# Attention probabilities kept side by side and turned in place, in a block of projections, dilated attention and HGRN2

## The chip, the cores and the metric

The kernel runs on one core of one Trainium2 chip. The metric is the device time of one execution in microseconds; lower is better. Engines are called as the profile calls them: PE is TensorE's matmuls and PEld its weight loads, DVE is VectorE, ACT is ScalarE, POOL is GpSimd, and SP issues most DMAs.

## What is computed

One layer of a hybrid encoder on 1024 tokens of width 1024, all in float32:

```
h = layer_norm(x)
aq, ak, av, hq, hf_fwd, hf_bwd, hi, hg, ga, gh = split(h @ w_in)          # 11776 columns
att = dilated_attention(aq, ak, av)    # 3 groups of 8 heads of 64: windows 128, 512, 2048 at dilation 1, 4, 16
rec = hgrn2(hq, hf_fwd, hf_bwd, hi, hg)   # 8 heads of 128: two gated linear recurrences, in chunks of 64
m = sigmoid(ga) * (att @ w_att_up) + sigmoid(gh) * (rec @ w_hgrn_up)
h = layer_norm(alpha * h + m @ w_o)
out = layer_norm(alpha * h + (silu(gate) * up) @ w_ffn_out)               # gate, up = split(h @ w_ffn_in)
```

Each attention group is a banded softmax with a linear bias in the distance. The three groups of a head are mixed with weights made of their softmax denominators: with each group's probabilities p, their row maximum and their row sum l, the output is the sum over the groups of w_g * (p_g @ v_g), where w_g holds one factor per query, exp(smallest shift - shift_g) over the common denominator.

HGRN2 has for each head and direction a cumulated product of the forget gate within a chunk, queries and keys scaled by it and by its reciprocal, a state that is carried from chunk to chunk, and the outputs of both directions added.

## The kernel before

The program has three phases. The change touches the first alone, `phase1`, which makes all 11776 columns of the input projection and, in between, the attention and the recurrences.

**The stream of products.** `stream` makes the projection in a Strassen-like form: groups of four 128-column tiles, 14 products for each group, 322 in all. A product is 12 matmuls of 128x512 (`mm3`, lines 225 to 227: high x high, high x low, low x high parts of float32 in TensorE's float32r type). Each needs a weight block split into a high part on ACT (line 200) and a low part on POOL (line 204); blocks are loaded by SP one group ahead. Results go through four PSUM banks (`ps_pj`); ACT and DVE take them out, and SP stores them to scratch in DRAM.

**Side work.** While the stream runs, the loop at the end of `phase1` advances one generator at a time: a unit of side work. `yield n` means: go on after n more products; a negative number also lets the next unit's inputs be fetched (`hgrn_pre`, `att_pre`, `near_pre`). For each i of 0 to 3 the units are two HGRN2 heads (`hgrn_side`), the far attention of a pair of heads (`att_far`, dilations 4 and 16) and the near attention of that pair (`att_near`, dilation 1). A unit begins when the stream has made the tiles that it reads. The order in the program is not exactly that of the code: instructions are ordered by priority, which is the order of the code save for evictions of the stream (`high_priority`), and by the program's own estimate of when their inputs are there. Side work has four PSUM banks of its own (`ps_sd`), used in turn, and nine SBUF slots of 4 KB a partition (`slot`).

**Far attention.** Scores of dilation 4 for 8 blocks (4 rounds r, 2 halves h) of 128 queries and 192 keys (line 565), and of dilation 16 for 128 queries and 128 keys (line 581), with bias and row maximum in one DVE instruction (line 517). A block's 320 numbers stand side by side; 16 exponentials follow (line 595). Then, for each round, `turn` transposes: of dilation 16 four full 128x128 blocks for each of the two heads in every other round (line 614), and of dilation 4, for each head, a full block (619), a half-width piece of one half (620), a half-width piece of the other half by a plain matmul into the lower partitions (621), and a full block (622). `att_pt` copies each bank to a fresh buffer, on ACT or DVE. The output matmuls of the round follow (633, 638, 642), and the next round's `turn` behind them. At the end `to_rows0` (line 661) brings the negated maxima N12 and the sums L12 into the row order of the near unit, in two passes of four matmuls with 16 columns.

**Near attention.** Scores of eight row tiles (line 696; tile 0 has two 64-row pieces), exponentials (715), the mixing weights W12 and W0 (lines 722 to 731), a broadcast of each on POOL (733), transposes (748 to 754) with copies, output matmuls (785). `weigh` transposes a broadcast weight (764) and multiplies: the far output OL and a copy ON of the near output are weighted apart and then added on POOL (796).

**A head of HGRN2.** `hgrn_dir` makes for each direction the gates, two scans (858), two reciprocals of 512 columns (866, 869) and the scaled queries and keys. Then: turn v; turn the keys of direction 0 (`hgrn_keys`, 884, 885); its state matmuls and state chain (`hgrn_states`, 900 to 912, the chain on DVE as hR and on ACT as hS); the same for direction 1; scores (`hgrn_scores`, 925 to 929) and outputs (`hgrn_out`, 951) for the two halves; the transposed store.

A plain float32 matmul shows as two PE instructions in the trace, a transpose as one.

Of the kernel before, what the change touches and what calls it, by code (L numbers as in the profile page):

```python
# [75 lines left out]
SMT_PAD = 640  # L76
# [3 lines left out]
class Block:  # L80
# [458 lines left out]
    FAR = [(s, o) for s in (2, 3, 4, 5, 8) for o in range(3)] + [(9, 0)]  # L539
# [5 lines left out]
    def att_far(self, j, qk):  # L545
# [3 lines left out]
        M1, M2, M12, N12, L12 = (self.att_small(n) for n in ("M1", "M2", "M12", "N12", "L12"))  # L549
# [3 lines left out]
        tiles = {n: self.slot(n, "pf", (3, 320)) for n in (2, 3, 4, 5, 8)}  # L553
        tiles[9] = self.smt.tile([128, 1, 320], F32, name="pf", tag="pf", bufs=1)

        def P(c, hd):
            s, o = self.FAR[2 * c + hd]
            return tiles[s][:, o, :]

        yield 2  # L560
        for r in range(4):
# [5 lines left out]
            for hd, ps in enumerate(pss):  # L567
                for h in range(2):
                    s, c = slice(192 * h, 192 * h + 192), 2 * r + h
                    self.ttr(P(c, hd)[:, 0:192], ps[:, s], bias[hd][:, s], M1[:, hd, c:c + 1])  # L570
            if r % 2:
                yield 1
        k2 = k2.rearrange("p (h r i m) -> p r i h m", h=2, r=4, i=4)
        for b in range(2):
# [8 lines left out]
            for hd, ps in enumerate(pss):  # L583
                for jj in range(4):
                    c, h = 4 * b + jj, jj % 2
                    self.ttr(P(c, hd)[:, 192:320], ps[:, jj, :], bias2[hd][:, 128 * h:128 * h + 128], M2[:, hd, c:c + 1])
            if b == 0:
                yield 1
# [14 lines left out]
        self.turned(V2, lambda kt: V2[:, kt, :])  # L603
        yield 1

        kw = dict(skip_group_check=True)
        t2 = {}

        def turn(r):
            if r % 2 == 0:  # L610
                for hd in range(2):
                    ps = self.ps_sd()
                    for jj in range(4):
                        nc.tensor.transpose(ps[:, 128 * jj:128 * jj + 128], P(2 * r + jj, hd)[:, 192:320], ident)
                    t2[hd] = self.att_pt(ps, 0, 512, hd).rearrange("p (r h c) -> p r h c", r=2, h=2)
            t = []
            for hd in range(2):
                ps, a, b = self.ps_sd(), P(2 * r, hd), P(2 * r + 1, hd)
                nc.tensor.transpose(ps[:, 0:128], a[:, 0:128], ident)
                nc.tensor.transpose(ps[0:64, 128:256], a[:, 128:192], ident)  # L620
                nc.tensor.matmul(ps[64:128, 128:256], b[:, 0:64], ident, start=True, stop=True)
                nc.tensor.transpose(ps[:, 256:384], b[:, 64:192], ident)
                t.append(self.att_pt(ps, 0, 384, hd))
            return t

        t = turn(0)
        yield 1
        O = [self.ps_sd(), self.ps_sd()]
        for r in range(4):
            o = [[O[h][HD[hd], 128 * r:128 * r + 128] for hd in range(2)] for h in range(2)]  # L630
            for h in range(2):
                for hd in range(2):
                    nc.tensor.matmul(o[h][hd], V1[:, 2 * r + h, HD[hd]], t[hd][:, 256 * h:256 * h + 128],
# [870 lines left out]
```

## Time and profile before

| | before |
|---|---|
| runs, median of 3 | 2222.41 us (2219.23 to 2223.08) |
| the profiled execution | 2221.32 us, span 2219.5 us |
| TensorE's mean granted clock | 0.98 |
| `w_lo` splits on POOL for the projection's blocks (line 204, wa) | 276, 1383 ns each |
| reciprocals of HGRN2 (lines 866 and 869) | 32, 3328 and 3333 ns each |
| exponentials of the far units (line 595) | 64, 551 ns each |

How to read it: the page gives the busy time of each engine, the chain of work that ended last, and groups of instructions by line with their mean length. Matmuls are pipelined, so the length of one (0.39 us for a product's matmul) is more than the time between two of them (0.23 us). The durations used below are taken from one profiled execution and set against that execution's own 2221.32 us.

### The profile page before, as it was taken

To read this page: it belongs to the slowest core of one execution; us is meant where nothing else is said; L and a number is where in the kernel's file an instruction comes from. 1 tells how busy PE (TensorE), PEld (TensorE's weight loads), DVE (VectorE), ACT (ScalarE), POOL (GpSimd) and SP (SyncE) were. 2 spreads that over 40 slices of the span, in tenths; PEclk is the share of its full clock that TensorE was granted. 3 is DMA by queue.
4 is the path that set the end of the run, shared out by engine and by line. 5 is a ranking of instruction groups with operands and counts; after the bars stand their busy time and mean duration, and the time that the engine had idled before them with its cause. 6 is when DMAs were issued, how large, how long until landed. Compare 5 with 4: busy or idle time off the path is not lost.

```text
span 2219.5 us, 30900 instructions
## 1 busy us (share of the span) xinstructions
PE 2111.7 (95%) x11105; PEld 1713.1 (77%) x11105; DVE 1223.2 (55%) x1917; ACT 883.2 (40%) x1744; POOL 1124.1 (51%) x911
## 2 busy tenths in 40 slices
PE   4799999998999999989999899998999999999998
PEld 3678877787777887777877788786788888887887
DVE  7666534785338852678424723248667676743221
ACT  6544445443544435544355432133444444432000
POOL 3465643665436763466543664446556665633120
PEclk9899999999999999999999999999999999999999
DMA  6333432434324443333432774334434443467453
GB/s 208 104 119 114 145 119 96 133 115 143 121 91 133 133 150 101 127 115 117 152 100 81 268 240 155 100 128 140 154 118 139 130 146 129 142 214 218 128 166 95
DMA packets 291643, 306.87 MB, mean 138 GB/s; under 512 B 14689, under 2 KB 222882, under 8 KB 291490
## 3 DMA queue, kind: packets, MB, share of 16 engines
q1 hardware_dynamic: 283744, 278.45, 39.7%
q10 hardware_dynamic: 7746, 26.45, 3.1%
q8 instruction: 87, 1.43, 0.3%
q14 instruction: 66, 0.54, 0.1%
HBM read 203.13 MB, written 101.71 MB: 137 GB/s over the span
## 4 chain that ended last, share of the span: by engine, by line
PE 66%; DVE 6%; DMA 4%; issue 3%; POOL 2%; ACT 1%; SPq 0%; DVEq 0%; ACTq 0%; POOLq 0%
PE pj L227 14%; PE pj L225 14%; PE pj L226 13%; PE sd L225 6%; PE sd L227 6%; PE sd L226 6%; DMA w_raw<-in_w_ffn_out_dram 2%; PE sd L951 1%; POOL w_lo L204 1%; PE sd L696 1%; DVE hR L912 1%; DMA t_raw<-td 1%; PE sd L785 1%; DVE wolo L204 1%; PE sd L509 1%
## 5 line engine op out<-in xcount | busy, mean ns | idle before, releaser
L204 POOL TENSOR_TENSOR w_lo<-wa,w_hi 128x512 fp32r<-128x512 f32 x276 | 379.9, 1383 | 318.1 <-ACT w_hi L200 294.2
L200 ACT CAST w_hi<-wa 128x512 fp32r<-128x512 f32 x276 | 170.3, 618 | 266.7 <-PE pj L226 193.6
L204 POOL TENSOR_TENSOR w_lo<-wsum,w_hi 128x512 fp32r<-128x512 f32 x88 | 122.0, 1398 | 129.3 <-ACT w_hi L200 77.4
L225 PE MATMUL pj<-xt1hi,w_hi 128*128 128x512 f32 x268 | 109.3, 408 | 27.2 <-ACT xt1hi L200 22.5
L204 POOL TENSOR_TENSOR w_lo<-f_raw,w_hi 128x512 fp32r<-128x512 f32 x66 | 99.7, 1511 | 46.2 <-ACT w_hi L200 43.9
L227 PE MATMUL pj<-xt1hi,w_lo 128*128 128x512 f32 x268 | 108.3, 405 | 1.9 <-POOL w_lo L204 1.9
L226 PE MATMUL pj<-xt1lo,w_hi 128*128 128x512 f32 x268 | 108.3, 404 | 0.3 <-DVE xt1lo L204 0.3
L225 PE MATMUL pj<-xb22hi,w_hi 128*128 128x512 f32 x268 | 105.8, 395 | 0.1
L227 PE MATMUL pj<-xb22hi,w_lo 128*128 128x512 f32 x268 | 105.8, 395 | 0.0
L226 PE MATMUL pj<-xb22lo,w_hi 128*128 128x512 f32 x268 | 104.9, 391 | 0.0
L200 ACT CAST w_hi<-wsum 128x512 fp32r<-128x512 f32 x88 | 54.6, 621 | 109.5 <-PE sd L226 74.3
L194 POOL TENSOR_TENSOR mv<-mv,mhalf 128x1 f32<-128x1 f32 x24 | 14.0, 586 | 165.2 <-DVE mv L193 164.2
L415 POOL TENSOR_TENSOR wa<-wa,wa 128x512 f32<-128x512 f32 x46 | 64.3, 1399 | 62.5 <-DVE ws L414 48.7
L204 POOL TENSOR_TENSOR w_lo<-ws,w_hi 128x512 fp32r<-128x512 f32 x46 | 65.2, 1419 | 60.7 <-ACT w_hi L200 53.0
L437 ACT COPY wkeep<-pj 128x512 f32<-128x512 f32 x138 | 80.2, 582 | 19.2 <-DVE evh L356 8.2
L225 PE MATMUL pj<-xb11hi,w_hi 128*128 128x512 f32 x188 | 76.3, 407 | 7.9 <-ACT xb11hi L200 7.9
L225 PEld LDWEIGHTS pj<-xt1hi,w_hi 128*128 128x128 f32 x268 | 52.3, 195 | 40.5 <-ACT xt1hi L200 23.0
L329 DVE TENSOR_TENSOR evh<-wkeep,pj 128x512 f32<-128x512 f32 x66 | 58.3, 886 | 44.3 <-PE pj L227 35.9
L903 ACT ACTIVATE hS<-hR,dec 128x128 f32<-128x128 f32 x112 | 44.6, 403 | 84.5 <-DVE hR L912 51.1
L225 PE MATMUL pj<-xt2hi,w_hi 128*128 128x512 f32 x188 | 74.8, 399 | 3.3 <-ACT w_hi L200 2.4
L225 PE MATMUL pj<-xt4hi,w_hi 128*128 128x512 f32 x188 | 75.3, 401 | 1.7 <-DVE wkeep L354 1.7
L248 ACT ACTIVATE y<-y,mv 128x1024 f32<-128x1024 f32 x14 | 17.3, 1244 | 148.3 <-DVE mv L247 93.1
(399 smaller groups left out, 6605.4 us busy)
## 6 DMA issues: line engine op xcount, KB each, us to landing
wa<-in_w_in_dram SPq DMA_DIRECT2D x184, 256.0 KB, 3.0
f_raw<-in_w_ffn_in_dram SPq DMA_DIRECT2D x44, 512.0 KB, 4.0
w_raw<-in_w_ffn_out_dram SPq DMA_DIRECT2D x22, 512.0 KB, 3.7
tg<-evh SPq DMA_DIRECT2D x32, 256.0 KB, 3.5
tg<-tg SPq DMA_DIRECT2D x16, 512.0 KB, 4.1
y<-ahs SPq DMA_DIRECT2D x16, 512.0 KB, 4.0
ah<-xt ACTq DMA_DIRECT2D x8, 512.0 KB, 4.6
rec<-hg ACTq DMA_DIRECT2D x8, 512.0 KB, 2.7
```

The costliest lines, as they stand in the source:

```text
L200: nc.scalar.copy(hi, src)
L204: e.tensor_sub(lo, src, hi.bitcast(F32))
L225: nc.tensor.matmul(ps, whi, xhi, start=first, stop=False, **kw)
L226: nc.tensor.matmul(ps, whi, xlo, start=False, stop=False, **kw)
L227: nc.tensor.matmul(ps, wlo, xhi, start=False, stop=last, **kw)
L329: nc.vector.tensor_tensor(o, self.order_src(add, g, kind), s, OP.add)
L415: nc.gpsimd.tensor_sub(a["a21"], a["a11"], a["a21"])
L437: nc.scalar.copy(t, ps)
L509: nc.tensor.transpose(ps[:, 128 * k:128 * (k + 1)], cols(4 * b + k), self.ident)
L696: nc.tensor.matmul(ps[:, tt % 2, :], q[pb, 128 * tt - 64:128 * tt + 64], k[pb, 128 * (tt - 1):128 * (tt + 1)], start=True, stop=True)
L785: nc.tensor.matmul(O[bank][HD[hd], c0:c1], V[:, kt, HD[hd]], t[hd][:, s0:s0 + c1 - c0], start=first, stop=(kt == 7), **kw)
L903: nc.scalar.activation(S[:, c, :], E, AF.Copy, scale=dec[:, 1, c:c + 1])
```

## The change

Three things are done.

In the far units a round's probabilities of dilation 4 stand side by side as 384 columns for both halves, with dilation 16 on either side of them where the slot has room (then one exponential still covers 320 columns) and in the upper part of another slot where not (then two exponentials, their sums added through LB). They are turned as full 128x128 blocks, three for dilation 4 and two for dilation 16, and copied back over themselves. All transposes come first, in three steps, and all outputs in one step. N12 and L12 are one tile NL and go through `to_rows0` in one pass of 32 columns.

In the near units the weight W0 is multiplied into the probabilities before they are turned, the weight W12 alone is broadcast and turned, the unused quarters of tile 0 are set to zero so that all its blocks are full, and the outputs are made row tile by row tile in one step. OL is multiplied by the turned weight and the outputs are added to it from PSUM.

In the heads, `hgrn_dir` is a generator: each direction is emitted in two parts, with a product between the parts and between the directions. Reciprocals are made in two halves. v and the keys of direction 0 are turned in one step, the keys of direction 1 go with the states of direction 0, and the two halves of scores, of outputs and of the last transposes each go in one step.

```diff
-    def att_pt(self, ps, c0, c1, i):
-        t = self.half("pt")
+    def copied(self, i, o, s):
         if i % 2:
-            self.nc.scalar.copy(t[:, c0:c1], ps[:, c0:c1])
+            self.nc.scalar.copy(o, s)
         else:
-            self.nc.vector.tensor_copy(t[:, c0:c1], ps[:, c0:c1])
-        return t
+            self.nc.vector.tensor_copy(o, s)
...
-    FAR = [(s, o) for s in (2, 3, 4, 5, 8) for o in range(3)] + [(9, 0)]
+    FAR = [(s, 128, s, 0) for s in (2, 3, 4, 5, 8)] + [(2, 640, 5, 640), (3, 640, 8, 640), (4, 640, 9, 0)]
...
-        for c in range(8):
+        for r in range(4):
             for hd in range(2):
-                v = P(c, hd)
-                nc.scalar.activation(v, v, AF.Exp, bias=N12[:, hd, c:c + 1], scale=QSCALE, accum_out=L12[:, hd, c:c + 1])
-        v1, v2 = self.fetch(0, "v1", d["v", 1], True), self.fetch(1, "v2", d["v", 2])
+                s1, _, s2, _ = self.FAR[2 * r + hd]
+                for h in range(2):
+                    c = 2 * r + h
+                    if s1 == s2:
+                        todo = [(tiles[s1][:, 320 * h:320 * h + 320], L12)]
+                    else:
+                        todo = [(P1(r, hd)[:, 192 * h:192 * h + 192], L12), (P2(r, hd)[:, h], LB)]
+                    for v, l in todo:
+                        nc.scalar.activation(v, v, AF.Exp, bias=N12[:, hd, c:c + 1], scale=QSCALE,
+                                             accum_out=l[:, hd, c:c + 1])
+        nc.vector.tensor_add(L12, L12, LB)
...
+        def turn1(r):
+            for hd in range(2):
+                ps, p = self.ps_sd(), P1(r, hd)
+                for n in range(3):
+                    nc.tensor.transpose(ps[:, 128 * n:128 * n + 128], p[:, 128 * n:128 * n + 128], ident)
+                self.copied(hd, p, ps[:, 0:384])
+
+        def turn2(r0):
+            for hd in range(2):
+                ps = self.ps_sd().rearrange("p (r e c) -> p r e c", r=2, e=2)
+                for r in range(2):
+                    for e in range(2):
+                        nc.tensor.transpose(ps[:, r, e], P2(r0 + r, hd)[:, e], ident)
+                for r in range(2):
+                    self.copied(hd, P2(r0 + r, hd), ps[:, r])
+
+        turn1(0)
+        turn1(1)
         yield 1
+        turn1(2)
+        turn2(0)
+        yield 1
+        turn1(3)
+        turn2(2)
+        perm = self.half("perm")
+        nc.sync.dma_start(perm, self.tabs[:, 128:640])
+        yield 2
...
-            if r < 3:
-                t = turn(r + 1)
-                yield -1 if r == 1 else 1
...
+        self.far = None, *self.to_rows0(perm, NL)
...
-        RB = []
-        for n, w in ((1, W12), (2, W0)):
+        for w in (W0, W12):
             nc.vector.tensor_mul(w, w, L0)
-            RB.append(self.slot(n, "rb", (8, 2, 64)))
-            nc.gpsimd.tensor_copy(RB[-1], w.rearrange("p a t -> p t a")[:, :, :, None].to_broadcast([128, 8, 2, 64]))
-        yield 1
+
+        RB = self.slot(1, "rb", (8, 2, 64))
+        nc.gpsimd.tensor_copy(RB, W12.rearrange("p a t -> p t a")[:, :, :, None].to_broadcast([128, 8, 2, 64]))
+        for tt in range(8):
+            for hd in range(2):
+                for p, z in rows(tt, hd):
+                    nc.vector.tensor_scalar(z, z, W0[p, hd, tt:tt + 1], None, op0=OP.mult)
+        yield 2
...
+        for b in range(4):
             for hd in range(2):
                 ps = self.ps_sd()
...
+                for tt in (2 * b, 2 * b + 1):
+                    for e in (0, 128):
+                        o = 256 * (tt % 2) + e
+                        nc.tensor.transpose(ps[:, o:o + 128], tile(tt, hd)[:, e:e + 128], ident)
+                self.copied(hd, P[b][:, hd].rearrange("p t c -> p (t c)"), ps)
+            if b % 2:
+                yield b
...
         for b, src, dst in cols:
-            nc.scalar.copy(ON[:, dst], O[b][:, src])
+            nc.vector.tensor_mul(OL[:, dst], OL[:, dst], RL[b][:, src])
+        for b, src, dst in cols:
+            nc.vector.tensor_add(OL[:, dst], OL[:, dst], O[b][:, src])
+        nc.scalar.dma_start(self.att_d[j], OL)
         yield -1
-        weigh(1, ON)
-        nc.gpsimd.tensor_add(OL, OL, ON)
-        nc.scalar.dma_start(self.att_d[j], OL)
...
-        nc.vector.reciprocal(qd[:, :, far], A)
         nc.gpsimd.tensor_mul(t3[:, :, near], t3[:, :, near], R)
+        yield
+        for c in (slice(0, 4), slice(4, 8)):
+            nc.vector.reciprocal(qd[:, c, far], A[:, c])
...
-            self.hgrn_dir(h, d, st)
+            for _ in self.hgrn_dir(h, d, st):
+                yield 1
+            if d == 0:
+                yield 1
         sg = self.fetch(8, "hg", self.hg_d[h]["g"])
+        yield 1
+        vT = self.turned(v.rearrange("p (k d) -> p k d", k=8), lambda c: v[:, 128 * c:128 * c + 128])
+        k0 = self.hgrn_keys(st, 0)
+        yield 3
+        S = {0: self.hgrn_states(st, 0, k0, vT)}
+        k1 = self.hgrn_keys(st, 1)
+        yield 3
+        S[1] = self.hgrn_states(st, 1, k1, vT)
+        yield 3
+        am = [self.hgrn_scores(st, b) for b in range(2)]
+        yield -2
+        on = [self.hgrn_out(st, b, am[b], vT, S) for b in range(2)]
         yield 2
...
```

More of the change, by code (lines that the diff above doesn't have):

```diff
@@ L552, in att_far, with P1, P2 @@
         bias, bias2 = self.att_bias(j, 1), self.att_bias(j, 2)
[L553 to L558, printed above, removed]
+        tiles = {n: self.slot(n, "pf") for n in (2, 3, 4, 5, 8)}
+        tiles[9] = self.smt.tile([128, 256], F32, name="pf", tag="pf", bufs=1)
+        nc.gpsimd.memset(LB, 0.0)
+        def P1(r, hd):
+            s, o = self.FAR[2 * r + hd][:2]
+            return tiles[s][:, o:o + 384]
+        def P2(r, hd):
+            s1, _, s, o = self.FAR[2 * r + hd]
+            if s1 != s:
+                return tiles[s][:, o:o + 256].rearrange("p (e c) -> p e c", e=2)
+            return tiles[s][:, 0:1024].rearrange("p (e c) -> p e c", e=2)[:, :, 0:128]
         yield 2
@@ L603, in att_far @@
         self.turned(V2, lambda kt: V2[:, kt, :])
-        yield 1
-        kw = dict(skip_group_check=True)
[L607 to L627, printed above, removed]
+        yield 2
[15 more added lines that the diff above has]
+        turn1(1)
+        yield 1
+        turn1(2)
[5 more added lines that the diff above has]
+        nc.sync.dma_start(perm, self.tabs[:, 128:640])
+        yield 2
+        kw = dict(skip_group_check=True)
         O = [self.ps_sd(), self.ps_sd()]
@@ L652, in att_far, with to_rows0 @@
             nc.scalar.copy(dst, O[h].rearrange("p (r i u) -> p r i u", r=4, i=4))
-        yield 1
-        self.far = OL, self.to_rows0(perm, N12, "N12r"), self.to_rows0(perm, L12, "L12r")
-    def to_rows0(self, perm, src, name):
+        self.far = OL, *self.far[1:]
+        yield -1
+    def to_rows0(self, perm, src):
         nc = self.nc
@@ L758, in att_near @@
-        cols = ((0, slice(64, 512), slice(0, 448)), (1, slice(0, 512), slice(448, 960)), (0, slice(0, 64), slice(960, 1024)))
-        def weigh(i, o):
-            RL = [self.ps_sd(), self.ps_sd()]
-            for tt in range(8):
-                c = 128 * (tt % 4)
-                nc.tensor.transpose(RL[tt // 4][:, c:c + 128], RB[i][:, tt].rearrange("p a d -> p (a d)"), ident)
-            for b, src, dst in cols:
-                nc.vector.tensor_mul(o[:, dst], o[:, dst], RL[b][:, src])
-        t = turn(0)
@@ L769, in att_near @@
-        yield 1
-        O = [self.ps_sd(), self.ps_sd()]
-        for b in range(4):
-            for kt in (2 * b, 2 * b + 1):
-                o = 256 * (kt % 2)
-                c = 128 * (kt % 4)
-                if kt == 0:
-                    parts = [(0, 64, 256, 64, True)]
-                elif kt == 3:
-                    parts = [(0, 384, 512, 256, False), (1, 0, 128, 384, True)]
-                elif kt == 7:
-                    parts = [(1, 384, 512, 256, False), (0, 0, 64, 384, False)]
-                else:
-                    parts = [(kt // 4, c, c + 256, o, False)]
-                for bank, c0, c1, s0, first in parts:
-                    for hd in range(2):
-                        nc.tensor.matmul(O[bank][HD[hd], c0:c1], V[:, kt, HD[hd]], t[hd][:, s0:s0 + c1 - c0],
-                                         start=first, stop=(kt == 7), **kw)
-            if b < 3:
-                t = turn(b + 1)
-                yield 1
@@ L790, in att_near @@
-        weigh(0, OL)
-        ON = self.slot(6, "on")
+                for tt in (2 * b, 2 * b + 1):
[5 more added lines that the diff above has]
+                yield b
+        RL = [self.ps_sd(), self.ps_sd()]
+        for tt in range(8):
+            c = 128 * (tt % 4)
+            nc.tensor.transpose(RL[tt // 4][:, c:c + 128], RB[:, tt].rearrange("p a d -> p (a d)"), ident)
@@ new lines, in att_near @@
+        O = [self.ps_sd(), self.ps_sd()]
+        todo = []
+        for kt in range(8):
+            c = 128 * (kt % 4)
+            todo.append((kt, O[kt // 4], c + (64 if kt == 0 else 0), c + 128, kt, 192 if kt == 0 else 128))
+            t = kt + 1
+            todo.append((kt, O[t % 8 // 4], 128 * (t % 4), 128 * (t % 4) + (64 if t == 8 else 128), t % 8, 0))
+        begun = set()
+        for n, (kt, o, c0, c1, t, p0) in enumerate(todo):
+            for hd in range(2):
+                first, last = id(o) not in begun, all(id(z[1]) != id(o) for z in todo[n + 1:])
+                nc.tensor.matmul(o[HD[hd], c0:c1], V[:, kt, HD[hd]], tile(t, hd)[:, p0:p0 + c1 - c0],
+                                 start=first, stop=last, **kw)
+            begun.add(id(o))
```

97 lines of the change are left out of this document (36 added, 61 removed).

## The prediction

> **What bounds the kernel now.** I read the page's busy line and its chain first, then the table of stages in the stretch where the changed code runs (122 to 1222 us), then TensorE's waits, then TensorE's timeline, because a sum of busy times cannot price short matmuls that overlap one another.
>
> ```profile
> span 2219.5 us, 30900 instructions
> PE 2111.7 (95%) x11105; PEld 1713.1 (77%) x11105; DVE 1223.2 (55%) x1917; ACT 883.2 (40%) x1744; POOL 1124.1 (51%) x911
> ...
> PE 66%; DVE 6%; DMA 4%; issue 3%; POOL 2%; ACT 1%; SPq 0%; DVEq 0%; ACTq 0%; POOLq 0%
> ...
> 122.00:276.00 154.00, 150.21 (x884) 126.50 (x882) 95.78 (x130) 66.69 (x132) 93.60 (x85) 0.99 0.42 132
> 276.00:405.00 129.00, 128.92 (x819) 98.02 (x818) 55.28 (x171) 61.70 (x149) 50.16 (x43) 1.00 0.37 117
> 405.00:545.00 140.00, 129.38 (x777) 107.83 (x776) 106.68 (x128) 58.42 (x117) 92.39 (x86) 0.98 0.39 124
> 545.00:682.00 137.00, 137.00 (x856) 105.22 (x855) 55.10 (x171) 65.53 (x157) 59.62 (x52) 1.00 0.36 116
> 682.00:810.00 128.00, 122.75 (x761) 102.74 (x761) 97.81 (x126) 55.70 (x111) 89.17 (x83) 1.00 0.42 134
> 810.00:940.00 130.00, 130.00 (x832) 100.56 (x832) 61.98 (x174) 63.21 (x153) 56.40 (x45) 1.00 0.38 120
> 940.00:1090.00 150.00, 141.17 (x829) 119.02 (x828) 105.95 (x130) 62.10 (x124) 101.06 (x93) 0.97 0.40 129
> 1090.00:1222.00 132.00, 132.00 (x830) 100.74 (x829) 50.67 (x166) 64.86 (x155) 52.48 (x43) 1.00 0.30 94
> ```
>
> After the stage and its length the columns are PE, PEld, DVE, ACT and POOL busy. The stages alternate: two HGRN2 heads, then a far and a near attention unit, four times. In the attention stages TensorE is busy for 527.92 of 528 us while no other engine passes half of the stage (PEld is TensorE's own weight load). There the time is TensorE's issue time, and each microsecond of it that goes is gone from the span, as the projection products that fill the rest don't change in number. In the head stages TensorE idles 3.8 + 10.6 + 5.2 + 8.8 = 28.4 us and VectorE is busy for 62 to 76%. So I sum two things separately: TensorE time in attention, and waits in the heads.
>
> **Prices, from TensorE's timeline** (start, length, instruction; I use start to start, as lengths overlap).
>
> ```profile
> 317.02 0.39 PE L226 MATMUL pj<-xt2lo,w_hi 128*128 128x512 f32 x1
> 317.34 0.66 PE L633 MATMUL sd<-pt,v 128*64 128x128 f32 x8
> 317.83 0.63 PE L638 MATMUL sd<-pt,vt 128*64 128x64 f32 x16
> ...
> 318.77 0.33 PE L619 MATMUL sd<-tabs_sb,pf 128*128 128x128 f32 x1
> 318.94 0.27 PE L620 MATMUL sd<-tabs_sb,pf 128*64 128x128 f32 x1
> 319.14 0.43 PE L621 MATMUL sd<-tabs_sb,pf 128*64 128x128 f32 x2
> 319.51 0.33 PE L622 MATMUL sd<-tabs_sb,pf 128*128 128x128 f32 x1
> 319.67 0.27 PE L619 MATMUL sd<-tabs_sb,pf 128*128 128x128 f32 x1
> ...
> 320.43 0.48 PE L227 MATMUL pj<-xt2hi,w_lo 128*128 128x512 f32 x1
> ...
> 326.62 1.09 PE L614 MATMUL sd<-tabs_sb,pf 128*128 128x128 f32 x8
> 327.47 0.47 PE L226 MATMUL pj<-xt1lo,w_hi 128*128 128x512 f32 x1
> 327.78 0.39 PE L227 MATMUL pj<-xt1hi,w_lo 128*128 128x512 f32 x1
> ```
>
> A full 128x128 transpose costs (327.47 - 326.62)/8 = 0.106 us. The set of lines 619 to 622, which puts two half-width pieces into one block, costs 0.90 (318.77 to 319.67) and 0.76 (319.67 to 320.43), so 0.83 us: each change between the 128*128 and the 128*64 form takes about 0.2 us. Going from a product matmul into a 128*64 run costs about 0.09 (317.02 to 317.34 is 0.32, where neighbouring products stand 0.23 apart). A run of full transposes pays nothing to enter, and the 0.08 that the product behind it loses (327.47 to 327.78) is what its last transpose saves. So fewer, larger steps are worth little in themselves; what goes is the half-width pieces, the form changes, and whole instructions.
>
> **The sum, part by part (four units each).**
>
> *Far transposes.* Before, a unit has 8 sets (6.64 us) and 16 full transposes (1.70). After, turn1 has 24 and turn2 has 16 full transposes: 40 x 0.106 = 4.24. That is 4.1 a unit, **16.4** in all.
>
> ```profile
> 353.78 0.96 PE L661 MATMUL sd<-N,perm 128*128 128x16 f32 x8
> 354.59 1.04 PE L661 MATMUL sd<-L,perm 128*128 128x16 f32 x8
> ...
> 388.92 0.39 PE L226 MATMUL pj<-xt1lo,w_hi 128*128 128x512 f32 x1
> 389.24 1.08 PE L785 MATMUL sd<-pt,v 128*64 128x256 f32 x8
> 390.26 0.33 PE L750 MATMUL sd<-tabs_sb,p 128*128 128x128 f32 x1
> ...
> 391.62 0.50 PE L227 MATMUL pj<-xt1hi,w_lo 128*128 128x512 f32 x1
> ...
> 397.30 1.09 PE L764 MATMUL sd<-tabs_sb,rb 128*128 128x128 f32 x8
> 398.15 0.48 PE L227 MATMUL pj<-xt3hi,w_lo 128*128 128x512 f32 x1
> ```
>
> *Row order* (line 661): one pass of 32 columns for two of 16. A pass takes 0.81 (353.78 to 354.59). That the wider pass costs the same is my choice; at worst it costs double and nothing is gained. 0.9 a unit with the second's tail, **3.6**.
>
> *Far outputs and scores in one run each.* Three of four output entries go (0.27), and one of the dilation-16 score runs (0.09 in, about 0.2 out): between 0.3 and 0.8 a unit, taken as 0.55, **2.2**.
>
> *Near transposes.* The group with two 64-wide pieces takes 1.36 us (390.26 to 391.62) where eight full ones take 0.85: 0.5. The other such group I put at 0.2, as its pieces stand at the start of a run. 0.7 a unit, **2.8**. The second set of weight transposes (line 764) goes: 0.85 a unit, **3.4**.
>
> *Near outputs.* 32 matmuls for 20, with the same columns. Eight 256-wide instructions take 1.02 (389.24 to 390.26) including some 0.2 to leave the form, 0.051 per 128 columns; eight 128-wide ones take 0.49 (317.34 to 317.83), 0.061. Sixty such pieces: 0.6 lost. Three entries and exits fewer (0.29 each): 0.9 won. **1.2** in all, between -2 and 4.
>
> *Heads.* Two score runs become one: 0.2 to 0.4 a head, **1.6** over eight heads. Nothing else there is removed.
>
> Together 31.2 us of TensorE time.
>
> *What lies beside other work.* VectorE and ScalarE have room in the attention stages (the table). Far: a unit has 22 exponentials for 16, six more ScalarE instructions of about 0.55 us, one small VectorE add and one GpSimd memset; the copies out of PSUM are as many bytes in slightly more pieces. Near: VectorE gains 18 scalings of the probabilities and three adds out of PSUM, and loses three multiplies; ScalarE loses the three copies of the output; GpSimd loses one 1024-wide broadcast and one 1024-wide add and gains two memsets. Moved DMAs: v1 and v2 are now fetched ahead of the dilation-16 scores, where SP would wait only for the last read of q1 and k1; the permutation is fetched before the outputs. The near unit's prefetch (q0, k0, the bias on GpSimd) comes after all far outputs, and k0's slot is free only when these have been read. Behind it on SP stand weight blocks, which are fetched seven products ahead (12 matmuls 0.23 apart are 2.7 us, so some 19 us), so a hold of one 6 us output run is hidden. The prefetch itself has three products, 8 us. I cost all of it at nothing; without cover a late k0 would cost a few us a unit.
>
> *The waits in the heads.*
>
> ```profile
> PE sd L900 <- ACT hkT L885: 8.1, 7, 2.4
> PE sd L928 <- DVE hR L911: 7.0, 3, 3.7
> PE sd L925 <- DVE hR L911: 4.6, 3, 2.3
> ```
>
> The keys are now turned three products ahead of the state matmuls instead of one, so I let 5 of the 8.1 us go (all if nothing else is late, none if the queue order holds ScalarE's copy). The scores' wait for the state chain stays: from the first states to the second scores there are six products before and after. Halved reciprocals let an eviction pass half-way; VectorE's work is the same plus four fixed costs a head. I count nothing for it, bounded by a microsecond a head either way.
>
> *New wait: the first near transposes now need the scalings.*
>
> ```profile
> 368.52 1.03 PE L509 MATMUL sd<-tabs_sb,v 128*128 128x128 f32 x8
> ...
> 373.14 1.25 DVE L731 TENSOR_TENSOR W<-W,L 128x16 f32<-128x16 f32 x2
> ...
> 372.99 1.29 POOL L204 TENSOR_TENSOR w_lo<-wa,w_hi 128x512 fp32r<-128x512 f32 x1 [6.29 <-ACT w_hi L200]
> ...
> L912 DVE TENSOR_SCALAR hR<-hR,dec x96: 269/288/1314, 162.2 to 1048.4; 128x128 f32<-128x128 f32 x96
> ```
>
> The weights are ready at 374.39, 5.9 us after v was turned. A scaling is not in this trace; the nearest row, half as wide, takes 0.288 us at the median and up to 1.314. I take 0.41 unhindered and 0.6 with GpSimd in the way, ten of them before the first transposes: 5.9 + 6.0 = 11.9 us, against two products and v's turn, 6.3. In strict order that would be 5.6 us of waiting a unit, 22 in all. But TensorE does not wait in that order today:
>
> ```profile
> 298.66 1.04 PE L509 MATMUL sd<-tabs_sb,vt 128*128 128x128 f32 x8
> ...
> 309.90 0.60 PE L614 MATMUL sd<-tabs_sb,pf 128*128 128x128 f32 x4
> ```
>
> The far transposes were emitted one product (2.7 us) behind the turn of v2, stand in the program 10 us behind it, and the stage has no idle time: products were put ahead. I count 2 us in all, between 0 and 22.
>
> So 31.2 + 5 - 2 = 34.2. The profiled execution took 2221.32 us (span 2219.5, 1.8 around it), and the median of the runs is 1.1 more. **2221.3 - 34.2 = 2187.** Weighed against a rule: the Trainium skill, page "SBUF — State Buffer", section "Who interferes with whom", says that VectorE's fast scalings and GpSimd's reads take one port pair in turn, whoever starts first blocking the other for a whole instruction. The trace agrees: the pair of tiny multiplies at 373.14 lasted until GpSimd ended at 374.28. By the page alone every scaling could meet such a block, which is the third rival.
>
> **The rivals.**
>
> *Head waits shrink too.* With a reciprocal that no longer holds evictions for its full length, and keys early, most of the 23 us left of the 28.4 go: 2187 - 22 = 2165. For it: the longest waits stand behind VectorE. Against it: VectorE does no less.
>
> *Head waits grow.* Scores now ask for four PSUM banks at once, behind the last state chain. If each of eight heads waits as the longest did (3.7) instead of 11.6/8 = 1.45: 18 us, 2205.
>
> *Slower: scalings behind GpSimd.* Place: VectorE in the near unit; TensorE in emitted order. At 1.314 each, the first ten end 5.9 + 13.1 = 19.0 us after v's turn, 12.7 past the cover; the other eight need 10.5 against 4.5, 6 more. 18.7 x 4 = 75 us, 2262. It decides when the wait passes 34/4 = 8.5 a unit, a mean of 0.74 a scaling. Against it: GpSimd is busy for 39 to 44% in these stages, so only some meet it.
>
> *It doesn't do what it says.* The merged output runs change form as often, and new idle time takes the rest: 2218 to 2226.
>
> **Chances.** The forecast 0.56 (2176 to 2200); shrinking head waits 0.16 (2155 to 2176); growing ones 0.14 (2200 to 2216); slower 0.08 (2227 to 2262); no change 0.06. A measurement here can tell about 0.2%, 4.4 us. Faster: 0.56 + 0.16 + 0.14 = 0.86; same 0.06; slower 0.08. The range 2158 to 2214 leaves out the last two cases and the far ends of the head cases.
>
> **What would show it.** TensorE's instructions in the attention stages still without gaps, and those stages some 7 to 8 us shorter each; no 128*64 form among the transposes; the wait for hkT nearly gone. Wrong, if TensorE waits for VectorE in front of the near transposes, or the head stages grow as the others shrink.

## The result, and the profile after

| | before | after |
|---|---|---|
| median of 4 runs each, same chip | 2220.82 us (2219.15 to 2223.08) | 2166.59 us (2163.32 to 2174.34) |
| ratio after to before, 95% | | 0.976 [0.975, 0.977] |
| the profiled execution | 2221.32 us, span 2219.5 | 2165.47 us, span 2163.7 |

The change saves 54 us where 34 were forecast: inside the range, but outside the forecast's own case (2176 to 2200), and some terms of the sum were far off, in both directions. First the page after (its busy line and the chain's shares by engine):

```profile
PE 2055.7 (95%) x11073; PEld 1700.9 (79%) x11073; DVE 1259.5 (58%) x2033; ACT 879.7 (41%) x1788; POOL 1115.9 (52%) x915
...
PE 61%; DVE 5%; DMA 4%; POOL 3%; issue 3%; ACT 2%; SPq 0%; DVEq 0%; POOLq 0%; ACTq 0%
```

TensorE is busy 56.0 us less and is still the bound. Now the table of stages, cut at the same product matmuls as the eight stretches shown of before (length first, then PE, PEld, DVE, ACT and POOL busy):

```profile
124.40:273.10 148.70, 146.07 (x866) 123.08 (x867) 94.33 (x132) 65.50 (x129) 87.95 (x80) 1.00 0.43 136
273.10:392.70 119.60, 117.05 (x802) 96.59 (x801) 64.46 (x192) 60.43 (x158) 51.50 (x48) 0.99 0.40 126
392.70:527.70 135.00, 126.23 (x778) 107.03 (x777) 106.54 (x136) 58.78 (x119) 88.10 (x82) 0.97 0.38 122
527.70:659.00 131.30, 127.13 (x847) 104.17 (x846) 71.26 (x199) 66.81 (x169) 61.45 (x59) 0.99 0.39 127
659.00:783.90 124.90, 121.67 (x770) 103.41 (x769) 98.33 (x133) 53.79 (x110) 87.02 (x79) 1.00 0.44 140
783.90:903.60 119.70, 119.09 (x817) 97.90 (x816) 66.34 (x192) 60.78 (x159) 55.15 (x47) 1.00 0.39 126
903.60:1054.80 151.20, 141.78 (x837) 119.25 (x836) 104.90 (x139) 63.83 (x127) 99.98 (x93) 0.97 0.41 132
1054.80:1175.60 120.80, 120.20 (x821) 98.88 (x820) 62.03 (x186) 63.51 (x165) 55.08 (x42) 1.00 0.38 122
```

The attention stages (second, fourth, sixth, eighth) are 9.4, 5.7, 10.3 and 11.2 us shorter, 36.6 together, although TensorE now idles in them for 7.9 us, where it idled for 0.1. The head stages are 5.3, 5.0, 3.1 shorter and then 1.2 longer, 12.2 together. TensorE's waits in phase 1 (what waited, for what, us in all, times, the longest), before and after, as far as they are not shown yet:

```profile
PE pj L227 <- POOL w_lo L204: 2.9, 3, 1.9
PE pj L225 <- DVE wkeep L354: 1.7, 1, 1.7
```

```profile
PE sd L948 <- DVE hR L931: 8.2, 5, 3.8
PE sd L785 <- DVE p L771: 7.3, 6, 2.5
PE pj L227 <- POOL w_lo L204: 6.3, 5, 2.2
PE pj L225 <- DVE evh L329: 5.6, 5, 3.0
PE pj L225 <- DVE wkeep L354: 5.2, 1, 5.2
...
PE sd L920 <- ACT hkT L905: 1.7, 2, 1.2
```

Of the waits of before, the one for the turned keys (hkT) has gone from 8.1 to 1.7, and the one for the state chain (hR) from 11.6 to 8.2. New are 7.3 us of near transposes behind the scalings (line 771), and products that wait for evictions by VectorE (evh of line 329 and wkeep of line 354: 10.8 after, of before only wkeep's 1.7). Products also wait longer for GpSimd's splits (w_lo, 6.3 for 2.9).

**Every group summed from start to start.** The table below is worked out from TensorE's timeline: each matmul of a group counts until the next one starts, plus what the product matmuls ahead of and behind its steps take beyond the usual 0.2275 us. The last row but two is what products lose between products. It runs from the 27th product to the first matmul of phase 2. In this stretch the clock stood at half rate for 27.3 us both before and after.

| us | before | after | saved | forecast |
|---|---|---|---|---|
| far transposes | 34.7 | 17.8 | 16.9 | 16.4 |
| row order | 7.2 | 4.0 | 3.2 | 3.6 |
| far scores and outputs | 49.0 | 46.4 | 2.6 | 2.2 |
| near scores | 27.6 | 17.1 | 10.5 | 0 |
| near transposes with their wait | 19.0 | 26.3 | -7.3 | 2.8 - 2 |
| near outputs | 19.3 | 14.2 | 5.1 | 1.2 |
| transposes of the weights | 7.3 | 3.9 | 3.4 | 3.4 |
| heads, and all turns of v | 163.8 | 143.8 | 20.0 | 1.6 + 5 |
| products behind products | 22.5 | 31.5 | -9.0 | 0 |
| together | | | 45.4 | 34.2 |
| phases 2 and 3 | 922.3 | 912.4 | 9.9 | 0 |

### The profile page after: what moved, and what is told of

Same layout as the page of the kernel before. It is cut to its first block, busy times and chain, and to the rows that moved or that the text cites. A ratio compares the mean times of both kernels' runs of the same rounds, so it can differ in the third digit from the quotient of the medians.

```text
span 2163.7 us, 31002 instructions
## 1 busy us (share of the span) xinstructions
PE 2055.7 (95%) x11073; PEld 1700.9 (79%) x11073; DVE 1259.5 (58%) x2033; ACT 879.7 (41%) x1788; POOL 1115.9 (52%) x915
## 4 chain that ended last, share of the span: by engine, by line
PE 61%; DVE 5%; DMA 4%; POOL 3%; issue 3%; ACT 2%; SPq 0%; DVEq 0%; POOLq 0%; ACTq 0%
PE pj L225 13%; PE pj L226 13%; PE pj L227 13%; PE sd L225 6%; PE sd L227 6%; PE sd L226 6%; POOL w_lo L204 2%; DMA w_raw<-in_w_ffn_out_dram 2%; PE sd L971 1%; DMA wa<-in_w_in_dram 1%; ACT p L749 1%; DVE hR L932 1%; PE sd L785 1%; DVE wolo L204 1%; DVE p L771 1%
## 5 line engine op out<-in xcount | busy, mean ns | idle before, releaser
L204 POOL TENSOR_TENSOR w_lo<-wa,w_hi 128x512 fp32r<-128x512 f32 x276 | 384.7, 1401 | 271.6 <-ACT w_hi L200 252.4
L225 PE MATMUL pj<-xt1hi,w_hi 128*128 128x512 f32 x268 | 109.6, 410 | 30.7 <-ACT xt1hi L200 22.5
L437 ACT COPY wkeep<-pj 128x512 f32<-128x512 f32 x138 | 80.2, 581 | 17.8 <-DVE a L299 6.3
L227 PE MATMUL pj<-xt2hi,w_lo 128*128 128x512 f32 x188 | 74.5, 396 | 3.3 <-POOL w_lo L204 3.3
L248 ACT ACTIVATE y<-y,mv 128x1024 f32<-128x1024 f32 x14 | 17.3, 1244 | 147.6 <-DVE mv L247 118.9
L225 PE MATMUL pj<-xb21hi,w_hi 128*128 128x512 f32 x188 | 75.5, 403 | 0.9 <-ACT evh L327 0.5
```

The costliest lines, as they stand in the source:

```text
L204: e.tensor_sub(lo, src, hi.bitcast(F32))
L225: nc.tensor.matmul(ps, whi, xhi, start=first, stop=False, **kw)
L227: nc.tensor.matmul(ps, wlo, xhi, start=False, stop=last, **kw)
L437: nc.scalar.copy(t, ps)
```

## The experiments

Each run gives a median and its ratio to the kernel before, measured with it, with a 95% interval. "Group" means a row of the table above, made in the same way from one profiled execution of the run.

### The parts alone and in pairs

The far part alone (with `copied` and the new `to_rows0`), the near part alone, and the heads alone, each put into the kernel before:

```diff
+        self.far = None, *self.to_rows0(perm, NL)
...
+        self.far = OL, *self.far[1:]
+        yield -1
```

```diff
+                    nc.vector.tensor_scalar(z, z, W0[p, hd, tt:tt + 1], None, op0=OP.mult)
+        yield 2
```

```diff
-            self.hgrn_dir(h, d, st)
+            for _ in self.hgrn_dir(h, d, st):
+                yield 1
```

> The far units as after the change, near units and heads as before. Theory: TensorE's time in the far units falls by 23 us as it did in the full change (transposes 17, row order 3.5, output and score runs 2), and the near scores, whose code is as before, also get about 10 us cheaper, since after the one output step they start later, with PSUM banks and VectorE free: about 2188. Rival: the cheaper near scores come from the near unit's own new code: about 2198, with the near scores broken into runs of four instructions as before.

> The near units as after the change, far units and heads as before. Theory: weight transposes, output run and full-size transposes save about 11 us, and the wait for the 18 scalings in front of the transposes takes 8 to 11 us back: 2217 to 2225, no difference to speak of. Rival: the near unit alone brought the cheaper scores and its scalings are hidden: about 2201.

> The heads as after the change, attention as before. Theory: the waits for hkT in front of the state matmuls go (8 us), so do those of the runs that start late, about 20 us in all: 2200, with TensorE's wait for hR still there. Rival: VectorE sets the pace of a head, and what is taken from one wait comes back in another (wkeep, evh): 2215 or more.

Then the change without its near part (far and heads), and without its part in the heads (far and near):

> Far units and heads as after the change, near units as before. Theory: the near unit's gain (weights turned once, outputs in one run, about 11 us) and its new waits (near transposes behind the scalings, about 11 us) cancel, so this is within 5 us of 2166.6. Rival: near's gain counts as in the near-only kernel (13 us) and this is 2178 or more.

> Far and near units as after the change, heads as before. Theory: what the heads' new order takes from the waits for hkT and in the outputs (some 15 us) comes back half as products waiting for VectorE (evh, wkeep, 10 us in the full change): 2170 to 2176, with those product waits down by half. Rival: the heads' order is a loss beside the other two parts: 2160 or less.

The last four columns are of phase 1, in us: all attention groups, the heads' group, the products behind products, and the time that the clock stood at half rate.

| | median, us | ratio | attention | heads | products | half rate |
|---|---|---|---|---|---|---|
| before | 2220.82 | | 164.2 | 163.8 | 22.5 | 27.3 |
| far | 2170.38 | 0.977 [0.975, 0.979] | 129.3 | 157.0 | 15.2 | 3.4 |
| near | 2209.45 | 0.995 [0.993, 0.997] | 157.1 | 155.1 | 29.3 | 30.7 |
| heads | 2214.58 | 0.996 [0.995, 0.998] | 163.6 | 157.1 | 26.0 | 17.1 |
| far and heads | 2176.69 | 0.980 [0.979, 0.982] | 129.4 | 154.7 | 23.4 | 20.5 |
| far and near | 2173.31 | 0.979 [0.977, 0.980] | 130.2 | 158.5 | 21.2 | 17.1 |
| all three | 2166.59 | 0.976 [0.975, 0.977] | 129.7 | 143.8 | 31.5 | 27.3 |

The far part alone gives nearly all of it. It came out 18 us below the 2188 that had been expected of it, the near part between its two cases, and the heads at the edge of their rival (2215). The near part and the heads save 11 and 8 us alone by their ratios, but on top of the far part neither gains anything by itself, and both together gain 4 us with intervals that overlap. Seen from the other end they do count: without the near part the change loses 10.1 us (the expectation was that this part cancels itself, within 5 us), without the heads' part 6.7 (as expected), with intervals that don't overlap, the second only just. So the parts don't add up, and what one is worth depends on the others. The groups show where some of it went. What the near part saves in outputs and weights against the far run (6.5 us) it pays in its transposes (7.1 us). The heads' group falls from 157.0 (far) to 143.8 (all), and the products behind products rise from 15.2 to 31.5. Some of that last step is the clock: half of the difference in half-rate time between these two traces is 12 us. So how much of the heads' gain is really given back isn't settled by these traces. Why the heads' group falls that far only when all three parts are there stays open too.

### Half-width pieces put back

In the changed kernel, the middle block of each three is again made of two half-width pieces. Nothing else is touched; the steps stay as few and as large.

```diff
-                for n in range(3):
-                    nc.tensor.transpose(ps[:, 128 * n:128 * n + 128], p[:, 128 * n:128 * n + 128], ident)
+                nc.tensor.transpose(ps[:, 0:128], p[:, 0:128], ident)
+                nc.tensor.transpose(ps[0:64, 128:256], p[:, 128:192], ident)
+                nc.tensor.matmul(ps[64:128, 128:256], p[:, 192:256], ident, start=True, stop=True)
+                nc.tensor.transpose(ps[:, 256:384], p[:, 256:384], ident)
```

> The kernel after the change, with the middle block of each dilation-4 set turned again as two half-width pieces (a transpose and a plain matmul), all else as after. Theory: TensorE's form changes are the price: far transposes go from 15.5 to about 32 us, and the time from 2166.6 to 2183. Rival: the price was that of sets standing between output runs, and pieces in a run of their own cost little: 2172 or less.

2187.27 us, 0.985 [0.983, 0.986]: 20.7 us of the gain are gone, 4 more than expected. TensorE's timeline of this run, and that of the whole change at such a step (start, length, instruction):

```profile
331.84 0.27 PE L629 MATMUL sd<-tabs_sb,pf 128*128 128x128 f32 x1
331.94 0.27 PE L630 MATMUL sd<-tabs_sb,pf 128*64 128x128 f32 x1
332.14 0.43 PE L631 MATMUL sd<-tabs_sb,pf 128*64 128x128 f32 x2
332.51 0.33 PE L632 MATMUL sd<-tabs_sb,pf 128*128 128x128 f32 x1
332.67 0.27 PE L629 MATMUL sd<-tabs_sb,pf 128*128 128x128 f32 x1
```

```profile
582.86 0.82 PE L630 MATMUL sd<-tabs_sb,pf 128*128 128x128 f32 x6
583.52 1.04 PE L638 MATMUL sd<-tabs_sb,pf 128*128 128x128 f32 x8
```

A set with pieces takes 0.83 us (331.84 to 332.67), a set of three full blocks 0.33 (582.86 to 583.52 is two). For 32 sets that is 16.0 us; the group of far transposes goes from 17.8 to 34.1. The Trainium skill, "TensorEngine Tiling (Array Packing)", section "Key Properties", says that changing the tiling mode drains TensorE; it gives no price, and this run does: two changes of form and two PE instructions more (a plain float32 matmul shows as two) make 0.5 us. How the 0.5 divides between the change of form and the half-width instructions themselves isn't shown. Of the whole loss of 20.7 us the group has 16.3; the near transposes take 5.3 more here, the heads' group about 5 less, and phases 2 and 3 take about 4.5 more, for no reason that this run shows. So the largest term of the forecast was right in size, and the half-width pieces are what costs it, not the number or the place of the steps.

### Why near scores got cheaper

Their code is the same. Before, they stood right behind the row order (354.59) and came head by head (TensorE's timeline of before):

```profile
357.93 1.13 PE L696 MATMUL sd<-k,q 64*128 64x256 f32 x4
358.99 0.50 PE L227 MATMUL pj<-xb11hi,w_lo 128*128 128x512 f32 x1
...
362.28 1.14 PE L696 MATMUL sd<-k,q 64*128 64x256 f32 x8
363.35 0.50 PE L226 MATMUL pj<-xb11lo,w_hi 128*128 128x512 f32 x1
```

Four instructions of one head take 1.06 us (357.93 to 358.99), eight of both heads 1.07 (362.28 to 363.35). The two heads' rows lie in different halves of the partitions, and their matmuls run side by side only when they stand mixed in the same run. After the change all do, in eight runs of 12 or 16 (the first, in the same view of the changed kernel):

```profile
342.85 1.57 PE L733 MATMUL sd<-k,q 64*128 64x256 f32 x12
```

The far part alone does it, with the near unit as before: the group is 17.5 us there. One theory: the far part now ends with a pause, so that both heads' PSUM banks are free when the scores are placed. The rival: it is something else in the new far part. Two runs put a pause behind the row order into the kernel before, of three products and of eight:

```diff
         self.far = OL, self.to_rows0(perm, N12, "N12r"), self.to_rows0(perm, L12, "L12r")
+        yield 3
```

```diff
         self.far = OL, self.to_rows0(perm, N12, "N12r"), self.to_rows0(perm, L12, "L12r")
+        yield 8
```

> The kernel before, with a pause of three products between the far unit and the near one. In the kernel before, the near scores run in pieces of four matmuls of one head (1.1 us each), in the far-only kernel in pieces of eight and more with both heads (1.1 us for eight). Theory: that comes from the near unit starting while PSUM banks and VectorE are still taken by the far unit's end; with the pause the near scores' TensorE time falls from 23.8 to about 16 and the time to about 2212. Rival: it comes from the shorter far unit itself (one bank for the row order instead of two, other orders): near scores stay at 23 or more, and the time within 4 us of 2222.

> The kernel before, with a pause of eight products instead of three between the far unit and the near one. The pause of three left the near scores where they were, right behind the row order (354.50 to 356.28 us), since the far unit ran some 10 us behind its place in the code. Theory: once the near scores stand clear of the row order and find all four banks free, they run with both heads together: their TensorE time falls from 23.8 to about 16, their runs from 17 to about 8. Rival: the cheap near scores need the far unit's new use of banks (three in turn at its end instead of four), not the distance: 23 or more even when they stand clear.

Three products did nothing there: the first near score stands at 356.28, still right behind the rows at 355.30, and the scores of the full row tiles stay in 21 runs, as before. The time, 2215.2 us, 0.998 [0.997, 0.999], moved without that. With eight, TensorE's timeline reads:

```profile
355.67 1.04 PE L662 MATMUL sd<-L,perm 128*128 128x16 f32 x8
...
360.20 0.32 PE L694 MATMUL sd<-k,q 64*64 64x128 f32 x1
...
360.58 1.57 PE L697 MATMUL sd<-k,q 64*128 64x256 f32 x12
```

The distance opened from 1.0 to 4.5 us, the runs became those of the changed kernel in three of the four units (10 runs in all), and the group fell from 27.6 to 18.5 us. That the pause does it is shown; that it works through the PSUM banks is my reading. The whole kernel gained nothing, 2220.83 us, 0.9995 [0.998, 1.001]: a pause that long moves the units that follow, and waits came back in front of products; the longest row of its waits is

```profile
PE pj L225 <- DVE evh L329: 12.2, 5, 4.1
```

### The wait for the scalings

TensorE and then VectorE of the changed kernel in the first near unit (in brackets: idle time ahead of the instruction, and what ended it):

```profile
362.30 0.39 PE L225 MATMUL pj<-xb21hi,w_hi 128*128 128x512 f32 x1
364.16 0.44 PE L785 MATMUL sd<-tabs_sb,p 128*128 128x128 f32 x2 [1.47 <-DVE p L771]
365.68 3.30 PE L785 MATMUL sd<-tabs_sb,p 128*128 128x128 f32 x14 [1.08 <-DVE p L771]
368.63 0.69 PE L226 MATMUL pj<-xb21lo,w_hi 128*128 128x512 f32 x1
```

```profile
361.73 7.57 DVE L771 TENSOR_SCALAR p<-p,W 64x128 f32<-64x128 f32 x18
```

The transposes were placed as if the scaled probabilities were there, and TensorE waited. Sixteen transposes, 1.7 us of work, hold it from 362.69 to 368.63. The mean of a scaling, 7.57/18 = 0.42 us, hides what held it up. The first three scalings of each unit take 0.94 to 1.24 us, the other fifteen 0.28 to 0.35 and stand about 0.26 apart. Here are the first three of this unit one by one, and what GpSimd did at the time:

```profile
361.73 1.15 DVE L771 TENSOR_SCALAR p<-p,W 64x128 f32<-64x128 f32 x1
362.90 1.21 DVE L771 TENSOR_SCALAR p<-p,W 64x128 f32<-64x128 f32 x1
364.14 1.19 DVE L771 TENSOR_SCALAR p<-p,W 64x128 f32<-64x128 f32 x1
```

```profile
361.76 1.04 POOL L767 COPY rb<-W 128x1024 f32<-128x1024 f32 x1 [0.18 <-DVE W L764]
362.76 1.26 POOL L204 TENSOR_TENSOR w_lo<-wa,w_hi 128x512 fp32r<-128x512 f32 x1
363.98 1.26 POOL L204 TENSOR_TENSOR w_lo<-ws,w_hi 128x512 fp32r<-128x512 f32 x1
```

Each of the three ends just behind a GpSimd instruction (362.88 behind 362.80, 364.11 behind 364.02, 365.33 behind 365.24). From 365.24 GpSimd does nothing, and the scalings run free. In the third unit it also goes the other way: fourteen scalings follow one another without a hold, and a GpSimd split that starts among them takes 4.80 us instead of 1.26, ending 1.2 us behind the last of them (876.16):

```profile
872.51 4.80 POOL L204 TENSOR_TENSOR w_lo<-wa,w_hi 128x512 fp32r<-128x512 f32 x1 [0.41 <-ACT w_hi L200]
```

So TensorE's wait here is in the main one for scalings that GpSimd held, by these rows; no run takes the hold away alone. Nor did VectorE set the pace afterwards: the last twelve transposes stand 0.21 us apart, twice the usual 0.106, under a clock at half rate (last section). In the third and fourth unit the transposes start 3.3 us behind the first scaling, and TensorE idles there for 0.6 us each.

One run leaves the scalings out, another gives the second head's to ScalarE:

```diff
-        for tt in range(8):
-            for hd in range(2):
-                for p, z in rows(tt, hd):
-                    nc.vector.tensor_scalar(z, z, W0[p, hd, tt:tt + 1], None, op0=OP.mult)
```

```diff
+                    if hd:
+                        nc.scalar.activation(z, z, AF.Copy, scale=W0[p, hd, tt:tt + 1])
+                    else:
+                        nc.vector.tensor_scalar(z, z, W0[p, hd, tt:tt + 1], None, op0=OP.mult)
```

> The kernel after the change without the multiplication of the near probabilities by W0 (the near outputs are left unweighted). Theory: TensorE's waits in front of the near transposes (7.3 us idle, some 4 more hidden in the last product's length) go and nothing takes their place: 2155 to 2158. Rival: the transposes wait for the exponentials and the row sums as much as for the scalings, or the side work is ready earlier but products wait instead: 2165 or more.

> The kernel after the change with the scalings of the second head on ScalarE and those of the first on VectorE. Theory: TensorE waits in front of the near transposes because 18 scalings in a row on VectorE take longer than the program assumes; on two engines they take half as long, and most of the 11 us that leaving them out gave comes: 2156 to 2160. Rival: ScalarE, which has just made the exponentials and turns out the banks, is then late with these: 2164 or more.

Without them 2155.31 us, 0.970 [0.969, 0.972]: the scalings cost 11.3 us by the medians. Split between two engines 2157.29 us, 0.972 [0.970, 0.974], 9.3 us better than the change, with intervals that don't overlap. The group of near transposes is 26.3, 16.3 (left out) and 20.3 us (split); 19.0 before. So 9 of the 11 us are had by halving VectorE's part, and this kernel is faster than the one before and than the change. How much of that is the shorter row of scalings, and how much the holds that go with it (seven instead of twelve in the four units), no run separates. The wait isn't gone, though; its waits in phase 1:

```profile
PE sd L951 <- DVE hR L934: 8.6, 5, 4.4
PE pj L225 <- DVE evh L329: 5.9, 5, 3.3
PE pj L225 <- DVE wkeep L354: 4.1, 2, 2.4
PE sd L788 <- DVE p L774: 3.9, 2, 2.3
```

### What bounds the heads

One run emits both directions at once again, with whole reciprocals; everything else of the change stays. Another takes the split scalings and lets the scores come one product later, to take away the wait for hR.

```diff
             for _ in self.hgrn_dir(h, d, st):
-                yield 1
-            if d == 0:
-                yield 1
+                pass
         sg = self.fetch(8, "hg", self.hg_d[h]["g"])
-        yield 1
+        yield 4
...
-        for c in (slice(0, 4), slice(4, 8)):
-            nc.vector.reciprocal(qd[:, c, far], A[:, c])
+        nc.vector.reciprocal(qd[:, :, far], A)
```

```diff
         S[1] = self.hgrn_states(st, 1, k1, vT)
-        yield 3
+        yield 4
```

> The kernel after the change with both directions of a head emitted at once and whole reciprocals, the heads' steps otherwise as after. Theory: of the heads' part the earlier turn of the keys does the work, and the order of emission only moves VectorE's work about: within 4 us of 2166.6, TensorE's wait for hkT still small. Rival: the parts and halves let evictions and the first direction's keys pass, and without them products or keys wait more: 2172 or more.

> The kernel with half of the scalings on ScalarE (2157.3), and in a head four products instead of three between the states of direction 1 and the scores. Theory: the scores' wait for the state chain on VectorE (8.9 us idle, and the half-rate clock behind the long ones) shrinks with 2.7 us more in front of it, six waits of 0.5 to 4.4 us: 2150 to 2154. Rival: VectorE sets the pace of the head stages, and the chain is pushed back as far by other work or the products wait instead: 2156 or more.

At once: 2169.22 us, 0.977 [0.975, 0.978], against 0.976 [0.975, 0.977]: the parts and the halves can't be told from none, and the heads' group is 144.7 for 143.8. Within the heads' edit that leaves the joined steps with more products between them; by themselves they don't do it, as the heads alone (157.1) showed. Scores later: 2155.53 us, 0.971 [0.969, 0.973], where the split alone gave 0.972 [0.970, 0.974], no difference; 2150 to 2154 had been expected. The wait that was aimed at did go, and others came (the waits of this run, in the same columns):

```profile
PE pj L225 <- DVE evh L329: 8.0, 5, 2.7
PE pj L225 <- DVE wkeep L354: 7.4, 2, 4.6
...
PE sd L951 <- DVE hR L934: 1.9, 2, 1.1
```

hR fell by 6.7 us, the two evictions rose by 5.4. VectorE is busy for 63 to 79% of the head stages of the change (94.33 of 148.70 to 106.54 of 135.00). A wait of TensorE's for it that is taken away in one place turned up in another here. This run also bears on the scalings: GpSimd holds one in each unit instead of one or two, and the idle time in front of the near transposes is 0.9 us where the split alone has 3.9.

## Why the prediction was right, and where it was not

**Right: what bounds the kernel, and the price of the half-width pieces.** Far transposes, row order, far scores and outputs, and the weights' transposes were forecast at 25.6 us and measured at 26.1. Putting the pieces back cost in their group what they had been priced at (16.3 us). That the whole stayed inside the range owes something to luck: the terms below were off both ways, and the time came out in the band of a rival with a chance of 0.16.

**A size off, and a reason missed: the new wait.** "I count 2 us in all, between 0 and 22." It was about 10: without the scalings the group of near transposes is 10.0 us shorter, and the kernel 11.3. Of these, 7.3 us are idle time, and two of the four units then ran their transposes at half rate. TensorE waiting for VectorE in front of the near transposes was the prediction's own sign of being wrong, and it was there. The mean was forecast well (0.41, measured 0.42), but by luck: it is made of three held scalings and fifteen at 0.26 from start to start. The first ten took 5.5 us where the prediction has 6.0. The rival with scalings held by GpSimd did come for three of every eighteen; it needed a mean of 0.74 us to decide, and stayed below. (The pair at 373.14 in the prediction multiplies two tensors and is no scaling; the scalings above show the hold themselves.) Wrong was also the way from 22 to 2: that the far transposes had found cover before was taken to mean that products are put ahead of whatever is late. In two units the near transposes found cover, in two they didn't: the group's time is 8.2, 9.1, 4.5 and 4.5 us by unit. That the program's estimate leaves out the hold, and so put too few products ahead, would fit; it is my reading and not shown.

**Missed: near scores, 10.5 us.** The forecast says that "fewer, larger steps are worth little in themselves". That was read off full transposes, whose runs pay nothing to enter. For 64-row matmuls of two heads, what stands in the run decides whether they overlap. The row with four instructions as long as eight was in the trace of before; the forecast prices only groups that the diff touches. Near outputs are too low in the forecast as well (1.2 for 5.1, above its upper bound of 4). They follow another step directly now, so that none of their 18 entries is left, and the narrower instructions cost nothing: the group's own time, without entries and exits, fell from 17.3 to 13.8.

**Too low and then too high: heads.** 6.6 were forecast, the groups fell by 20.0, and 9.0 came back in front of products: net 11. The wait for the keys went by 6.4 (5 forecast). The reading that "VectorE does no less" held: TensorE idles in the head stages for 24.0 us, where it idled for 28.4. The rival by which most of these waits go names 2165, close to the result, but not for its reason. That each attention stage would be 7 to 8 us shorter and without gaps came out as 5.7 to 11.2 us with 7.9 us of gaps.

**Not in any term: 9.9 us in code that the change doesn't touch.** From the first matmul of phase 2 on (1297.2 us before, 1251.3 after), the same 3929 matmul instructions take 922.3 and 912.4 us in the two profiled executions. In the fourteen profiled executions of this study they take between 911 and 922 us, with 13.7 to 23.9 us of half-rate clock in them, 23.9 before and 17.1 after. At half rate half of the time is lost, so the clock explains 3.4 of the 9.9 us. Where the rest goes, and whether it belongs to the change, stays open: the medians differ by 54.2, more than the 45.4 of phase 1.

## What to carry to other kernels

Price a step by the forms of its pieces as the trace shows them, not by its number of instructions: two half-width pieces between full blocks took 0.6 us where one full block takes 0.1. When a change puts work of another engine in front of TensorE, cost it in strict order unless something shows that other work is put ahead, ask one by one which of its instructions some other engine will hold (a mean hides them), and see whether the work can be split between two engines. Then look one unit further in the queue: code that isn't in the diff can gain or lose as much by its new distance to the step ahead.

## What the runs showed of the hardware

The clock answers to a single wait. In the changed kernel TensorE waited 3.77 us for the state chain; its timeline behind that wait, and two windows around it (behind POOL's busy time stands the granted clock, 1.00 and 0.51):

```profile
950.01 0.37 PE L948 MATMUL sd<-qd,t 128*64 128x64 f32 x1 [3.77 <-DVE hR L931]
...
953.79 0.63 PE L225 MATMUL pj<-xb11hi,w_hi 128*128 128x512 f32 x1
954.22 0.63 PE L226 MATMUL pj<-xb11lo,w_hi 128*128 128x512 f32 x1
```

```profile
942.50:949.30 6.80, 3.74 (x55) 3.02 (x53) 6.52 (x14) 3.64 (x8) 3.03 (x2) 1.00 0.48 161
949.30:956.20 6.90, 6.19 (x43) 5.31 (x44) 4.11 (x9) 3.31 (x8) 3.27 (x4) 0.51 0.60 218
```

Products stand 0.43 us apart instead of 0.23 until 956.28, so the wait cost about 3 us more than its own length. One long wait isn't needed. Where the first near transposes begin, TensorE was busy for 0.85 of 3.40 us with no idle time longer than 1.47, and the next 3.40 us ran at half rate (the same columns):

```profile
362.30:365.70 3.40, 0.85 (x5) 0.23 (x3) 3.34 (x5) 0.87 (x2) 2.95 (x3) 0.99 0.34 97
365.70:369.10 3.40, 3.40 (x15) 3.32 (x16) 3.40 (x14) 0.00 (x0) 0.00 (x0) 0.50 0.19 58
```

The Trainium skill, "TensorE: Matmul & The Clock Gate", Part 1, says that the clock halves after an idle window of about 3.4 us and stays so until a busy one has passed, with windows that run free of the program. The trace agrees that it halves behind idle time, but the second case shows that a window need not be idle throughout. After the long wait full speed came 6.3 us behind the first matmul (950.01 to 956.28), so nearly two such windows; in the second case it came after one. Half-rate time in phase 1 lay between 3.4 and 34.1 us in these profiles, which is why the traces of two kernels are compared here by groups, and whole kernels by medians.
